# A two-layer hybrid decoder step: decode and projection buffers shared slot by slot, and other places in the order for steps of the mixers

## Chip, core and metric

The kernel runs on one core of a Trainium2 chip. The metric is the device time of one execution in microseconds (us). Engines: PE (TensorE, matmuls; PEld its weight loads), DVE (VectorE), ACT (ScalarE), POOL (GpSimd), SP (SyncE, which issues nearly all DMAs here; SPq is its queue).

## What is computed

One inference step of a two-layer trunk: 1024 prompt tokens and 8 sequences of 4 new tokens each. In each layer

```python
proj = x @ w_in                       # one input projection, 46 chunks of 128 columns here
# SSD (Mamba-2, 16 heads), MLA (latent attention, 8 heads, 8192 cached rows for each of the 8 sequences), GDN (gated DeltaNet, 4 heads)
mix = jnp.concatenate([y_ssd, y_mla, y_gdn], axis=-1)          # width 2048
x_new = layer_norm(DEEPNORM_ALPHA * x + mix @ w_out, ln_g, ln_b)
```

All of it is float32. The large products (input projection, q and kv of MLA, output projection) are three matmuls on a high and a low part of each operand: a `split` is a cast on ACT (high part) and a subtraction (low part) on DVE or POOL.

## The kernel before

Tokens are columns, in three blocks of 384, 384 and 288. Each layer has two phases.

**Phase 1** (`phase1`) interleaves three generators on PE: stream a (MLA norms, two GDN heads, one SSD group), stream b (layer norm of the input, two GDN heads, the sample's GDN, the other SSD group) and a filler (input projection, then `mla_q`, `mla_kv`, `absorb`). `merge` writes PE's order out by hand: a step that yields a number asks to be resumed that many us of the planner's PE clock (`self.clock`) later, a step that yields a set waits for those chunks, and the filler runs whenever no stream is due. The other engines' orders are made by a list scheduler (program order as priority, by its own estimates); `high_priority` moves what is traced inside it ahead. Queues of all engines are in order. PSUM banks in phase 1: `pj` 2 (filler), `a` 3, `b` 3.

Steps the change touches in phase 1: `rstd` (second half of a norm, two matmul groups with DVE and POOL L318 between), `gdn_block` (chains of small products whose results DVE takes from PSUM: L153, L829, L836), `ssd` (B and C products, copied out by ACT at L1024), `ssd_sample` (state update, first of eight after `stack`), `mla_q` (loads latents into `cq`; `product` writes bank `pj`; results go to DRAM as `qd`), and the end of the filler: `mla_prompt` loads queries for the attention, `absorb` loads `w_ukT` and four pieces of `qd` and makes the decode's queries, `mla_kv` makes keys and values.

**Phase 2** (`phase2`) first weaves the decode (32 units: gather 256 KB of rope rows and 2 MB of latents through POOL's queue, transpose them on DVE, scores `ps_dS`, softmax, `ps_dV`) with the prompt's attention (`mla_prompt`, banks `aS`, `aT`, `aO`); `weave_decode` fixes the orders of PE and DVE: every yield of the decode is a number of us for which attention steps run. `decode_end` joins the parts of the decode. Then the output projection `out_proj`: for each block of tokens 8 chunks of 48 matmuls, each chunk with two halves of weights `wo` (512 KB each, split), and 16 pieces `mix` (split) for the block; `ps_m` has 3 banks, `wo` 5 buffers of which a chunk uses 4. A `layer_norm` follows each block. The decode's buffers are one pool, the projection's another that takes the same memory after the first is closed. What attention is left after the decode is woven with the first block's projection (`weave`, 0.7 us of projection for 1 us of attention).

Of the kernel before, what the change touches and what calls it, by code (L numbers as in the profile page):

```python
# [33 lines left out]
SHARE2 = 0.7  # L34
# [93 lines left out]
class Builder:  # L128
# [177 lines left out]
    def rstd(self, T, tag, ss, n, mul, eps, soon=contextlib.nullcontext):  # L306
# [12 lines left out]
        yield 2.98  # L319
# [198 lines left out]
    def phase1(self, l):  # L518
# [3 lines left out]
        with self.pool(f"p1{l}") as p, self.psum_pool(f"p1ps{l}", pj=2, a=3, b=3):  # L522
# [32 lines left out]
            def fill():  # L555
# [27 lines left out]
            a = Stream([{0}], misc, self.gdn_head("a", 0), self.gdn_head("a", 2), self.mla_in("a"), self.ssd("a", 0))  # L583
# [116 lines left out]
    def gdn_block(self, r, L, T, Q, h, nb, x, S, ahead):  # L700
# [121 lines left out]
        for c, w in enumerate(ws):  # L822
# [6 lines left out]
            nc.vector.tensor_copy(out=vn, in_=p[:, :128])  # L829
# [5 lines left out]
            if S is None:  # L835
                nc.vector.tensor_copy(out=Sn, in_=p[:, :128])  # L836
            else:
                e = (16 + h) * 16 + cc + c
                self.stt(Sn, S, self.elast[:, e:e + 1], p[:, :128], ALU.mult, ALU.add)
# [5 lines left out]
        yield 5.2  # L845
# [160 lines left out]
    def ssd(self, r, g):  # L1006
# [9 lines left out]
        for t0 in (0, 4, 8):  # L1016
            p, p2 = self.psum(r), self.psum(r)
# [5 lines left out]
            if t0 < 8:  # L1023
                nc.scalar.copy(out=Bt[:, t0 * 128:t0 * 128 + 512], in_=p)  # L1024
                self.tt(nc.vector, CB[:, t0 * 128:t0 * 128 + 512].rearrange("p (c n) -> p c n", c=4), p2.rearrange("p (c n) -> p c n", c=4),
                        self.const[:, C_INC:C_INC + 128].unsqueeze(1).to_broadcast([128, 4, 128]))
            else:
                nc.scalar.copy(out=Bt[:32, 1024:1152], in_=p[:32, :128])
                self.tt(nc.vector, CB[:32, 1024:1056], p2[:32, :32], self.const[:32, C_INCS:C_INCS + 32])
# [107 lines left out]
    def ssd_sample(self, r, X, T, g, CT, Bt, CB, acc, big):  # L1137
# [55 lines left out]
        for b in range(8):  # L1193
            if b == 4:
                old((6, 7))
            yield 2.03
# [57 lines left out]
    def mla_q(self, cq, rot, ck, T):  # L1254
# [12 lines left out]

        def product(w, nb):
            n = BLOCKS[nb][1]
            ps = self.psum("pj")  # L1270
# [131 lines left out]
    def phase2(self):  # L1402
        l = self.l
        last = l == DEPTH - 1
        W, mla = self.regA[:, 0:4672], self.mla
        with self.psum_pool(f"p2ps{l}", aS=2, aT=2, aO=1):
            with self.pool(f"p2d{l}") as pd, self.psum_pool(f"p2dp{l}", dV=1) as ps:
                kts = self.hole.tile([128, 4224], F32, name="dec_k", tag="hole", bufs=1)

                V = {k: pd.tile([128, 4096], F32, name=f"dec_v{k}") for k in (2, 0, 1)}  # L1410
                self.RV = itertools.cycle([V[k] for k in range(3)])
                dec = self.decode(Ring(pd.tile([128, 8304], F32, name="dec")), kts, ps)
                self.weave_decode(dec, mla)
            with self.pool(f"p3{l}") as p3, self.psum_pool(f"p3ps{l}", m=3):

# [4 lines left out]
                ws = self.out_weights(itertools.cycle(rw), Ring(self.regA, 4672))  # L1420
                Rt = self.cso[:, 0:384]
                Ry = [p3.tile([128, 3072], F32, name="y"), W[:, 1536:4608]]
# [3 lines left out]
                self.pkv.close()  # L1426
                if not last:
                    self.take_x(l + 1)
                T = Ring(W, 0, 1536)
                Rx = Ring(self.tq(F32))  # L1430
                par = self.par[l]
                for nb in range(3):
                    if nb:
                        x2 = nb == 2 and not last
                        y = self.mix_load(Rx, Rm, None if x2 else Ry[nb % 2], None if x2 else Rt, nb)
                        out = self.out_proj(ws, nb, *y)
                    for _ in out:
                        pass
                    if last or nb < 2:
# [543 lines left out]
```

## Time and profile before

| | us |
|---|---|
| median of 3 runs | 3574.2 (3568.78 to 3581.75) |
| profiled execution, its time | 3572.76 |
| profiled execution, its span from first to last instruction | 3571.0 |
| PE busy | 3124.5 |
| mean granted PE clock | 0.939 of 2.4 GHz |
| layer 0: phase 1, decode, projection | 0 to 1060, 1060 to 1540, 1540 to 1800 |
| layer 1: phase 1, decode, projection | 1800 to 2816, 2816 to 3300, 3300 to 3555 |

A row of a timeline gives start, length, engine, line and operation as out<-in, with the number of merged instructions; a bracket gives the idle time before it and what ended that. A row of waits gives the engine and its line, what it waited for, us in total, times, and the longest.

### The profile page before, as it was taken

What the parts mean: (1) busy time and instruction counts of PE and PEld (TensorE: products, weight loads), DVE (VectorE), ACT (ScalarE), POOL (GpSimd) and SP (SyncE); (2) the same over time, 40 slices, a digit from 0 to 9 for tenths busy, and PEclk for the clock granted to TensorE, in tenths of its full rate; (3) what the DMA queues carried; (4) which work ended last, traced back from release to release, by engine and by line L of the source; (5) the groups of instructions that cost most, each with busy time, mean ns of one, the idle gap of its engine ahead of it and who ended that gap; (6) DMA issues with size and microseconds to landing.
All of it is one profiled execution on the core that took longest, in us unless ns stands there. A gap on an engine that the chain in (4) does not pass through costs nothing. (4 is left out here: it accounts for less than half of the span.)

```text
span 3571.0 us, 82553 instructions
## 1 busy us (share of the span) xinstructions
PE 3124.5 (87%) x33880; PEld 2666.9 (75%) x33880; DVE 2234.9 (63%) x4646; ACT 1337.2 (37%) x3099; POOL 1124.5 (31%) x1214
## 2 busy tenths in 40 slices
PE   6889999888778988979979999898987788889797
PEld 5888988888665655559878899887886566556697
DVE  7766365687545766745586653657865466666455
ACT  5433234333133344434434332343322343434344
POOL 4434344644421211101134444355453111211000
PEclk7999999999888999989989999999998799999898
DMA  3322324555776655444424232255567755553453
GB/s 137 123 90 88 106 67 161 168 169 177 249 251 201 207 178 191 171 154 157 151 83 126 83 94 90 68 171 184 173 214 254 230 191 190 183 196 128 161 180 127
DMA packets 317070, 564.70 MB, mean 158 GB/s; under 512 B 51772, under 2 KB 218748, under 8 KB 299668
## 3 DMA queue, kind: packets, MB, share of 16 engines
q1 hardware_dynamic: 293140, 408.42, 35.9%
q0 software_dynamic: 23552, 151.01, 12.0%
q8 instruction: 266, 4.36, 0.5%
q14 instruction: 112, 0.92, 0.1%
HBM read 429.00 MB, written 130.30 MB: 157 GB/s over the span
## 5 line engine op out<-in xcount | busy, mean ns | idle before, releaser
L180 PE MATMUL ps_pj<-xh,w_r 128*128 128x384 f32 (+1 forms) x4416 | 1212.7, 342 | 50.8 <-ACT p_cv L471 17.2
L180 PEld LDWEIGHTS ps_pj<-xh,w_r 128*128 128x128 f32 x4416 | 816.1, 196 | 71.0 <-ACT p_cv L471 19.1
L180 PE MATMUL ps_pj<-xl,w_r 128*128 128x384 f32 (+1 forms) x2208 | 733.9, 332 | 4.6 <-POOL xl L153 4.0
L180 PEld LDWEIGHTS ps_pj<-xl,w_r 128*128 128x128 f32 x2208 | 432.4, 196 | 13.5 <-POOL xl L153 11.1
L180 PE MATMUL ps_m<-mix,wo 128*128 128x384 f32 (+1 forms) x2304 | 395.4, 333 | 44.1 <-DVE wo L153 19.3
L180 PEld LDWEIGHTS ps_m<-mix,wo 128*128 128x128 f32 x2304 | 385.4, 196 | 50.8 <-DVE wo L153 22.4
L156 DVE SCALAR_TENSOR_TENSOR p_cv<-p_cv,c 128x384 f32<-128x384 f32 (+1 forms) x432 | 335.0, 779 | 71.9 <-ACT p_cv L159 65.9
L180 PE MATMUL ps_dS<-dec_k,c 32*32 32x256 f32 x8192 | 314.7, 385 | 31.5 <-issue 12.8
L153 POOL TENSOR_TENSOR w_r<-w_raw,w_r 128x1024 fp32r<-128x1024 f32 (+1 forms) x98 | 233.2, 2379 | 293.5 <-ACT w_r L165 251.3
L180 PEld LDWEIGHTS ps_dS<-dec_k,c 32*32 32x32 f32 x8192 | 190.1, 106 | 135.7 <-issue 85.0
L1667 DVE STREAM_TRANSPOSE dec_k<-dec_v 128x2048 f32<-128x2048 f32 x128 | 290.9, 2282 | 0.1
L1643 POOL DMA_INDIRECT dec<-cache_k_rope,c x64 | 60.9, 951 | 566.0 <-DVE dec L1736 516.9
L153 DVE TENSOR_TENSOR wo<-c,wo 128x1024 fp32r<-128x1024 f32 x96 | 119.0, 1243 | 128.2 <-PE ps_m L180 98.3
L159 ACT ACTIVATE p_cv<-p_cv 128x384 f32<-128x384 f32 x144 | 72.8, 505 | 314.8 <-DVE p_cv L156 313.8
L1470 ACT COPY c<-ps_aT 128x512 f32<-128x512 f32 (+3 forms) x192 | 89.9, 478 | 248.0 <-PE ps_aT L150 241.2
L165 ACT CAST wo<-c 128x1024 fp32r<-128x1024 f32 x96 | 100.4, 1050 | 218.3 <-DMA c<-w_out 174.9
L1643 POOL DMA_INDIRECT dec_v<-cache_kv_latent,c x128 | 120.8, 943 | 182.9 <-PE ps_dV L180 157.6
L180 PE MATMUL ps_b<-p_b 128*128 128x128 f32 (+7 forms) x1476 | 156.8, 284 | 21.1 <-ACT p_b L1024 8.4
L1513 DVE TENSOR_REDUCE c<-ps_aS 128x1 f32<-128x512 f32 (+3 forms) x192 | 105.4, 549 | 101.7 <-PE ps_aS L180 96.3
L159 ACT ACTIVATE c<-ps_aS,c 128x512 f32<-128x512 f32 (+3 forms) x192 | 110.6, 576 | 153.7 <-DVE c L1514 138.6
L318 POOL TENSOR_TENSOR c<-c,c 128x3 f32<-128x3 f32 (+2 forms) x22 | 17.1, 783 | 472.6 <-DVE c L317 472.6
L180 PEld LDWEIGHTS ps_b<-p_b 128*128 128x128 f32 (+5 forms) x1476 | 133.6, 161 | 37.7 <-ACT p_b L1024 9.9
(325 smaller groups left out, 5601.6 us busy)
## 6 DMA issues: line engine op xcount, KB each, us to landing
c<-w_out SPq DMA_DIRECT2D x96, 512.0 KB
w_raw<-w_in SPq DMA_DIRECT2D x92, 512.0 KB
pd<-p_cv SPq DMA_DIRECT2D x164, 192.0 KB
p_b<-pd SPq DMA_DIRECT2D x66, 256.0 KB
c<-pd SPq DMA_DIRECT2D x64, 256.0 KB
q<-rowd SPq DMA_DIRECT2D x48, 256.0 KB
p_b<-rowd SPq DMA_DIRECT2D x48, 256.0 KB
pd<-p_cv SPq DMA_DIRECT2D x82, 144.0 KB
```

The costliest lines, as they stand in the source:

```text
L153: eng.tensor_tensor(out=out, in0=a, in1=b, op=op)
L156: self.nc.vector.scalar_tensor_tensor(out=out, in0=a, scalar=s, in1=b, op0=op0, op1=op1)
L159: self.nc.scalar.activation(out=out, in_=in_, func=func, **kw)
L165: self.nc.scalar.copy(out=hi, in_=src)
L180: return self.nc.tensor.matmul(out, lhsT=lhsT, rhs=rhs, start=start, stop=stop)
L318: nc.gpsimd.tensor_tensor(out=r[:p, u], in0=r[:p, u], in1=self.mhalf[:p, 0:1].to_broadcast([p, u.stop - u.start]), op=ALU.pow)
L1470: nc.scalar.copy(out=t[:, :w], in_=p[:, :w])
L1513: nc.vector.reduce_max(out=m, in_=ps[:, :w], axis=AX.X)
L1643: nc.gpsimd.indirect_dma_start(out=out, out_offset=None, in_=src, in_offset=bass.IndirectOffsetOnAxis(ap=idx[:, c:c + 1], axis=0))
L1667: nc.vector.transpose(T[r].rearrange("p j s k -> p j (s k)"), V[:, :, r * 128:r * 128 + 128])
```

## The change

- `rstd`, the last step of `gdn_block`, the first state update of `ssd_sample` and the second and third group of `ssd` yield larger numbers, so their next PE instructions are put later in PE's order. DVE and ACT instructions of the GDN chains and of `ssd` get high priority.
- `mla_q` loads two blocks of latents before the rotation table; its products alternate between banks `pj` and `a`.
- `absorb` starts (and loads) before `mla_prompt`; the filler waits there until stream a has ended.
- In phase 2 one pool holds slots v0, v1, v2, d1, d2, d3. The projection's tiles take a slot each: `wo` takes v2, `mix` v0, v1 and d1, `y` takes d2. The first two halves of `w_out` are loaded (through `tok`) and split after unit 29, the first five `mix` after unit 30, eleven after the last; these splits subtract on POOL. The decode's first three loads come together, with no attention before the first unit.
- An attention step counts for at least 0.45 us in `weave_decode`. `decode_end` is woven with attention and the projection's first chunk. `ps_m` uses the banks of `dS` and `dV`, later of `aS` too. `wo` has 4 buffers in place of 5, its raw loads 3 in place of 2, its later splits high priority.

```diff
-        yield 2.98
+        yield 5.5
...
-            while due > 0 and next(second, self) is not self:
+            while due > 0:
+                if next(second, self):
+                    break
                 due, t = due - (self.clock - t), self.clock
...
-                    due -= self.clock - t
+                    due -= max(self.clock - t, 0.45)
...
+                yield {"a"}
+                absorb = self.absorb()
+                next(absorb)
                 self.mla = self.mla_prompt(self.tq(F32R), self.regA[:, 0:4672])
                 next(self.mla)
-                absorb = self.absorb()
-                next(absorb)
...
-            a = Stream([{0}], misc, self.gdn_head("a", 0), self.gdn_head("a", 2), self.mla_in("a"), self.ssd("a", 0))
+            def end():
+                self.done.add("a")
+                yield from ()
+            a = Stream([{0}], misc, self.gdn_head("a", 0), self.gdn_head("a", 2), self.mla_in("a"), self.ssd("a", 0), end())
...
-            self.tt(nc.vector, c3(Xc), c3(p), mk1(C_L1 + 32 * lv))
+            with self.tc.high_priority():
+                self.tt(nc.vector, c3(Xc), c3(p), mk1(C_L1 + 32 * lv))
...
-            self.tt(nc.vector, Tc, Tc, p, ALU.subtract)
-            nc.vector.transpose(Uc, Tc)
+            with self.tc.high_priority():
+                self.tt(nc.vector, Tc, Tc, p, ALU.subtract)
+                nc.vector.transpose(Uc, Tc)
...
-            nc.vector.tensor_copy(out=vn, in_=p[:, :128])
+            with self.tc.high_priority():
+                nc.vector.tensor_copy(out=vn, in_=p[:, :128])
...
+            with self.tc.high_priority():
+                if S is None:
+                    nc.vector.tensor_copy(out=Sn, in_=p[:, :128])
+                else:
+                    e = (16 + h) * 16 + cc + c
+                    self.stt(Sn, S, self.elast[:, e:e + 1], p[:, :128], ALU.mult, ALU.add)
...
-        yield 5.2
+        yield 7.5
...
         for t0 in (0, 4, 8):
+            if t0:
+                yield 2.5
             p, p2 = self.psum(r), self.psum(r)
...
+            with self.tc.high_priority():
+                if t0 < 8:
+                    nc.scalar.copy(out=Bt[:, t0 * 128:t0 * 128 + 512], in_=p)
+                    self.tt(nc.vector, CB[:, t0 * 128:t0 * 128 + 512].rearrange("p (c n) -> p c n", c=4), p2.rearrange("p (c n) -> p c n", c=4),
...
-            yield 2.03
+            yield 2.03 if b else 7.0
...
+        banks = itertools.cycle(("pj", "a"))
         def product(w, nb):
             n = BLOCKS[nb][1]
-            ps = self.psum("pj")
+            ps = self.psum(next(banks))
...
-        tables = {2: table(2, self.cst[:, 0:288], self.cst[:, 288:576]), 0: table(0, rot[:, 0:384], self.cso)}
+        tables = {2: table(2, self.cst[:, 0:288], self.cst[:, 288:576])}
         yield {"latents"}
-        for nb in (2, 0, 1):
-            latents(nb)
+        latents(2)
+        latents(0)
+        tables[0] = table(0, rot[:, 0:384], self.cso)
+        latents(1)
...
-        with self.psum_pool(f"p2ps{l}", aS=2, aT=2, aO=1):
-            with self.pool(f"p2d{l}") as pd, self.psum_pool(f"p2dp{l}", dV=1) as ps:
-                kts = self.hole.tile([128, 4224], F32, name="dec_k", tag="hole", bufs=1)
-                V = {k: pd.tile([128, 4096], F32, name=f"dec_v{k}") for k in (2, 0, 1)}
-                self.RV = itertools.cycle([V[k] for k in range(3)])
-                dec = self.decode(Ring(pd.tile([128, 8304], F32, name="dec")), kts, ps)
-                self.weave_decode(dec, mla)
-            with self.pool(f"p3{l}") as p3, self.psum_pool(f"p3ps{l}", m=3):
-                wo = lambda k: p3.tile([128, 1024], F32R, name=f"wo{k}")
-                rw = [wo(k) for k in range(4)]
-                Rm = itertools.cycle([p3.tile([128, 384], F32R, name=f"mix{k}") for k in range(32)])
-                rw.append(wo(4))
...
-                y = self.mix_load(None, Rm, Ry[0], Rt, 0)
-                out = self.out_proj(ws, 0, *y)
-                self.weave(mla, out, SHARE2)
...
+        with self.psum_pool(f"p2ps{l}", aS=2, aT=2, aO=1, dV=1) as ps, self.pool(f"p2d{l}") as pd:
+            kts = self.hole.tile([128, 4224], F32, name="dec_k", tag="hole", bufs=1)
+            place = lambda t, n, dt, name: pd.tile([128, n], dt, name=name, tag=t, bufs=1)
+            self.RV = itertools.cycle([lambda k=k: place(f"v{k}", 4096, F32, "dec_v") for k in range(3)])
+            d1, d2, d3 = (Ring(place(f"d{k}", n, F32, f"dec{k}")) for k, n in ((1, 4616), (2, 3072), (3, 608)))
+            d = {"T": [kts[:, r * 2048:r * 2048 + 2048].rearrange("p (j s k) -> p j s k", j=16, s=4) for r in range(2)],
+                 "gs": kts[:, 4096:4224], "ps": ps, "W": Ring(kts, 0, 4096)}
...
+            def projection():
+                rw = place("v2", 4096, F32R, "wo")
+                ws = self.out_weights(itertools.cycle([rw[:, k:k + 1024] for k in range(0, 4096, 1024)]), Ring(self.regA, 4672))
+                first = [next(ws), next(ws)]
+                yield
+                Rm, mix = [], [[], []]
+                for t, n, k0, k1 in (("v0", 4096, 0, 5), ("v1", 4096, 5, 10), ("d1", 4616, 10, 16)):
+                    m = place(t, n, F32R, "mix")
+                    Rm += [m[:, k * 384:k * 384 + 384] for k in range(2 * (k1 - k0))]
+                    self.mix_part(None, iter(Rm[2 * k0:]), 0, range(k0, k1), mix, nc.gpsimd)
+                    if t == "v0":
+                        yield
+                d.update(Rm=itertools.cycle(Rm), mix=mix, ws=itertools.chain(first, ws))
+            d["projection"] = projection()
+            self.weave_decode(itertools.chain(self.decode_setup(d1, d2, d3, d), self.decode_units(d)), mla)
+            next(d["projection"], None)
+            ws, Rm, y = d["ws"], d["Rm"], [d["mix"]]
+            two = lambda: ps.tile([128, 1024], F32, name="ps_m", tag="dS", bufs=1)
+            self.ms = itertools.cycle([two, lambda: self.psum("dV")])
+            def tail():
+                for _ in self.decode_end(d):
+                    for _ in itertools.islice(mla, 4):
+                        yield
+                Ry[0] = place("d2", 3072, F32, "y")
+                y.extend(self.mix_rest(Ry[0], Rt, 0))
+                yield from mla
+            out = self.out_proj(ws, 0, y)
+            self.weave(tail(), out, SHARE2)
+            self.pkv.close()
+            if not last:
+                self.take_x(l + 1)
+            T = Ring(W, 0, 1536)
+            Rx = Ring(self.tq(F32))
+            self.ms = itertools.cycle([two, lambda: self.psum("aS"), lambda: self.psum("dV"), lambda: self.psum("aS")])
+            par = self.par[l]
+            for nb in range(3):
+                if nb:
+                    x2 = nb == 2 and not last
+                    y = [self.mix_part(Rx, Rm, nb, range(16), [[], []], nc.vector)]
+                    y.extend(self.mix_rest(None if x2 else Ry[nb % 2], None if x2 else Rt, nb))
+                    out = self.out_proj(ws, nb, y)
+                for _ in out:
+                    pass
+                if last or nb < 2:
+                    finish(self.layer_norm("aT", T, y[1], nb, par[:, P_LNG:P_LNG + 8], par[:, P_LNB:P_LNB + 8], last,
+                                           self.total("aT", y[1], y[2]), Ry[nb % 2][:, :8 * BLOCKS[nb][1]]))
...
+    def decode_setup(self, D1, D2, D3, d):
...
-        vs, p5, O, m, al, sm, q4 = (D(n) for n in (256, 256, 2048, 32, 32, 32, 512))
+        (O, wv), (vs, p5, m, al, sm) = (D2(n) for n in (2048, 1024)), (D3(n) for n in (256, 256, 32, 32, 32))
         cks, krs, st = self.cso[:, 0:64], self.cso[:, 64:96], self.cso[:, 96:112]
-        d["load"], d["wv"] = self.decode_load(Ring(D(1536))), D(1024)
-        d["D"] = D.rest()
+        d["load"], d["wv"] = self.decode_load(Ring(D1(1536))), wv
+        q4 = D1(512)
+        d["D"] = D1.rest()
         d["ready"] = [d["load"](0, 0)]
-        yield 2.0
         self.dma(q4, self.qxd.rearrange("p r n -> p (r n)"))
         self.dma(cks.rearrange("p (r n) -> p r n", r=2), self.cks)
         self.dma(krs[0:32], self.krd[:, SEQ:NT])
         self.dma(d["gs"].rearrange("p (k n) -> p k n", k=4), self.gated[:, :, SEQ:NT])
         self.dma(d["wv"], self.i["w_uv"][l])
-        d["ready"] += [d["load"](0, 1)]
-        yield 2.0
-        d["ready"] += [d["load"](0, 2)]
+        d["ready"] += [d["load"](0, 1), d["load"](0, 2)]
+        yield 0.0
...
+            V, rr = next(RV)(), RR(512)
...
+            if k in (29, 30):
+                next(d["projection"])
...
-        W = Ring(d["D"].a, d["D"].base, d["D"].size)
+        W = d["W"]
...
+    def mix_part(self, Rs, Rm, nb, ks, mix, eng):
         c0, n, _ = BLOCKS[nb]
...
+        for k in ks:
             hi, lo = next(Rm)[:, :n], next(Rm)[:, :n]
             raw = Rs(384)[:, :n] if Rs else lo.bitcast(F32)
             self.dma(raw, self.mixd[:, k, c0:c0 + n])
             with self.tc.high_priority() if nb else contextlib.nullcontext():
-                self.split(None, raw, n, hi, lo, self.nc.vector)
+                self.split(None, raw, n, hi, lo, eng)
             mix[0].append(hi)
             mix[1].append(lo)
...
+        for k in range(48):
+            hi, lo = next(Rw), next(Rw)
+            raw = self.tok[:, :1024] if k < 2 or k % 3 == 0 else Rr(1024)
+            c, hf = k // 2 % 8, k % 2
+            self.dma(raw, self.i["w_out"][self.l, c, :, hf * 1024:hf * 1024 + 1024])
+            with self.tc.high_priority() if k > 1 else contextlib.nullcontext():
+                w = self.split(None, raw, None, hi, lo, self.nc.vector if k > 1 else self.nc.gpsimd)
+            yield w
...
+    def out_proj(self, ws, nb, parts):
         n = BLOCKS[nb][1]
+        mix = parts[0]
         for c in range(8):
             w = [next(ws), next(ws)]
-            ps = self.psum("m")
+            ps = next(self.ms)()
             for k in range(16):
                 hi, lo = w[k // 8]
                 s = slice((k % 8) * 128, (k % 8) * 128 + 128)
                 self.mm3(ps[:, :n], (hi[:, s], lo[:, s]), (mix[0][k], mix[1][k]), k == 0, k == 15)
                 yield
+            while len(parts) < 3:
+                yield True
+            y, total = parts[1:]
             self.stt(y[c], y[c], ALPHA, ps[:, :n], ALU.mult, ALU.add)
```

## Rows read from the trace of the kernel before

**Rows 1.** The page's first part: busy time and share of the span by engine.
```profile
PE 3124.5 (87%) x33880; PEld 2666.9 (75%) x33880; DVE 2234.9 (63%) x4646; ACT 1337.2 (37%) x3099; POOL 1124.5 (31%) x1214
```

**Rows 2.** Six stretches: length, busy PE, PEld, DVE, ACT, POOL (instructions), PEclk, DMA, GB/s.
```profile
1530.00:1640.00 110.00, 89.91 (x606) 75.77 (x591) 46.07 (x115) 37.99 (x64) 0.00 (x0) 0.88 0.47 162
3290.00:3400.00 110.00, 91.20 (x636) 76.58 (x621) 46.30 (x117) 38.40 (x64) 0.00 (x0) 0.89 0.44 152
1030.00:1110.00 80.00, 58.10 (x586) 42.72 (x587) 31.04 (x82) 27.49 (x81) 13.63 (x15) 0.77 0.69 211
2785.00:2870.00 85.00, 61.94 (x628) 45.64 (x626) 34.99 (x88) 28.98 (x85) 14.06 (x16) 0.74 0.69 208
940.00:1030.00 90.00, 70.35 (x409) 59.80 (x408) 52.58 (x107) 25.79 (x53) 33.27 (x38) 0.92 0.84 285
2695.00:2785.00 90.00, 69.16 (x385) 58.90 (x384) 50.06 (x103) 24.75 (x50) 29.63 (x35) 0.89 0.83 277
```

**Rows 3.** Waits of PE over the whole run: us in total, times, longest.
```profile
PE ps_m L180 <- DVE wo L153: 19.3, 10, 4.6
PE ps_pj L180 <- DMA cq<-cqd: 19.2, 4, 9.2
PE ps_a L180 <- ACT c L1024: 18.7, 2, 9.5
PE ps_a L180 <- DVE c L153: 18.4, 2, 9.5
PE ps_m L180 <- ACT mix L165: 17.9, 2, 9.9
...
PE ps_a L180 <- DVE p_sa L153: 15.3, 10, 5.3
...
PE ps_pj L180 <- DVE stage L153: 10.5, 7, 3.2
PE ps_b L180 <- DVE p_sb L153: 10.5, 12, 2.1
...
PE ps_a L180 <- DVE p_sa L829: 8.5, 6, 3.3
...
PE ps_b L180 <- ACT p_b L1024: 8.4, 2, 4.2
...
PE ps_a L150 <- DVE q L153: 7.0, 4, 3.3
...
PE ps_b L180 <- POOL p_b L318: 5.5, 4, 2.7
```

**Rows 4.** Timeline at the end of layer 0's decode: start, length, engine, line, operation, [idle before].
```profile
1556.15 9.32 PE L180 MATMUL ps_dV<-dec 128*32 128x256 f32 x32
...
1571.31 10.73 SPq L136 DMA_DIRECT2D mix<-mixd  x16
1578.12 8.33 ACT L165 CAST mix<-mix 128x384 fp32r<-128x384 f32 x16 [8.81 <-DMA mix<-mixd]
1578.66 8.38 DVE L153 TENSOR_TENSOR mix<-mix,mix 128x384 fp32r<-128x384 f32 x16 [7.29 <-ACT mix L165]
```

**Rows 5.** Timeline between phase 1 and decode, layer 0.
```profile
1025.06 8.34 SPq L136 DMA_DIRECT2D q<-qd  x14
...
1039.86 7.00 PE L180 MATMUL ps_a<-c 64*128 64x32 f32 x32 [8.93 <-DVE c L153]
...
1041.69 1.22 POOL L1643 DMA_INDIRECT dec_v<-cache_kv_latent,c  x1 [1.42 <-DMA c<-gated]
...
1060.89 0.95 POOL L1643 DMA_INDIRECT dec<-cache_k_rope,c  x1 [16.74 <-PE ps_aS L180]
```

**Rows 6.** Timeline of SP's queue where the MLA latents are loaded, layer 0.
```profile
966.90 0.51 SPq L136 DMA_DIRECT2D rot<-rotq  x1
967.47 4.70 SPq L136 DMA_DIRECT2D cq<-cqd  x6
```

**Rows 7.** One group by line: a 384-column subtraction on POOL, busy and mean ns.
```profile
L153 POOL TENSOR_TENSOR xl<-p_b,xh 128x384 fp32r<-128x384 f32 (+1 forms) x32 | 32.9, 1058 | 14.2 <-ACT xh L165 14.2
```

More of the change, by code (lines that the diff above doesn't have):

```diff
@@ L834, in gdn_block @@
             Sn = Q(128)
[L835 to L839, printed above, removed]
+            with self.tc.high_priority():
[4 more added lines that the diff above has]
+                    self.stt(Sn, S, self.elast[:, e:e + 1], p[:, :128], ALU.mult, ALU.add)
             S = Sn
@@ L1402, in phase2 @@
     def phase2(self):
-        l = self.l
+        nc, l = self.nc, self.l
         last = l == DEPTH - 1
         W, mla = self.regA[:, 0:4672], self.mla
-        with self.psum_pool(f"p2ps{l}", aS=2, aT=2, aO=1):
-            with self.pool(f"p2d{l}") as pd, self.psum_pool(f"p2dp{l}", dV=1) as ps:
-                kts = self.hole.tile([128, 4224], F32, name="dec_k", tag="hole", bufs=1)
-                V = {k: pd.tile([128, 4096], F32, name=f"dec_v{k}") for k in (2, 0, 1)}
-                self.RV = itertools.cycle([V[k] for k in range(3)])
-                dec = self.decode(Ring(pd.tile([128, 8304], F32, name="dec")), kts, ps)
-                self.weave_decode(dec, mla)
-            with self.pool(f"p3{l}") as p3, self.psum_pool(f"p3ps{l}", m=3):
-                wo = lambda k: p3.tile([128, 1024], F32R, name=f"wo{k}")
-                rw = [wo(k) for k in range(4)]
-                Rm = itertools.cycle([p3.tile([128, 384], F32R, name=f"mix{k}") for k in range(32)])
-                rw.append(wo(4))
-                ws = self.out_weights(itertools.cycle(rw), Ring(self.regA, 4672))
-                Rt = self.cso[:, 0:384]
-                Ry = [p3.tile([128, 3072], F32, name="y"), W[:, 1536:4608]]
-                y = self.mix_load(None, Rm, Ry[0], Rt, 0)
-                out = self.out_proj(ws, 0, *y)
-                self.weave(mla, out, SHARE2)
[L1426 to L1439, printed above, removed]
-                        finish(self.layer_norm("aT", T, y[1], nb, par[:, P_LNG:P_LNG + 8], par[:, P_LNB:P_LNB + 8], last,
-                                               self.total("aT", y[1], y[2]), Ry[nb % 2][:, :8 * BLOCKS[nb][1]]))
@@ L1577, in mla_prompt @@
         yield from pend
-    def decode(self, D, kts, ps):
-        d = {"T": [kts[:, r * 2048:r * 2048 + 2048].rearrange("p (j s k) -> p j s k", j=16, s=4) for r in range(2)],
-             "gs": kts[:, 4096:4224], "ps": ps}
-        yield from self.decode_setup(D, d)
-        yield from self.decode_units(d)
-        yield from self.decode_end(d)
-    def decode_setup(self, D, d):
+    def decode_setup(self, D1, D2, D3, d):
         nc, l = self.nc, self.l
-        vs, p5, O, m, al, sm, q4 = (D(n) for n in (256, 256, 2048, 32, 32, 32, 512))
+        (O, wv), (vs, p5, m, al, sm) = (D2(n) for n in (2048, 1024)), (D3(n) for n in (256, 256, 32, 32, 32))
         cks, krs, st = self.cso[:, 0:64], self.cso[:, 64:96], self.cso[:, 96:112]
-        d["load"], d["wv"] = self.decode_load(Ring(D(1536))), D(1024)
-        d["D"] = D.rest()
+        d["load"], d["wv"] = self.decode_load(Ring(D1(1536))), wv
+        q4 = D1(512)
+        d["D"] = D1.rest()
         d["ready"] = [d["load"](0, 0)]
-        yield 2.0
         self.dma(q4, self.qxd.rearrange("p r n -> p (r n)"))
@@ L1645, in load @@
         def load(b, u):
-            V, rr = next(RV), RR(512)
+            V, rr = next(RV)(), RR(512)
             for x in range(2):
@@ L1821, in decode_end @@
         self.dma(self.mixd[:, 8:12, SEQ:NT], y.rearrange("p (k n) -> p k n", k=4))
-    def mix_load(self, Rs, Rm, Ry, total, nb):
+    def mix_part(self, Rs, Rm, nb, ks, mix, eng):
         c0, n, _ = BLOCKS[nb]
-        mix = [[], []]
-        for k in range(16):
+        for k in ks:
             hi, lo = next(Rm)[:, :n], next(Rm)[:, :n]
@@ L1831, in mix_load, with mix_rest @@
             with self.tc.high_priority() if nb else contextlib.nullcontext():
-                self.split(None, raw, n, hi, lo, self.nc.vector)
+                self.split(None, raw, n, hi, lo, eng)
             mix[0].append(hi)
             mix[1].append(lo)
+        return mix
+    def mix_rest(self, Ry, total, nb):
+        c0, n, _ = BLOCKS[nb]
         if Ry is None:
@@ L1842, in mix_load @@
             y = [y[:, c] for c in range(8)]
-        return mix, y, total[:, :n]
+        return y, total[:, :n]
     def out_weights(self, Rw, Rr):
-        def load(c):
-            for hf in range(2):
-                raw = Rr(1024)
-                self.dma(raw, self.i["w_out"][self.l, c, :, hf * 1024:hf * 1024 + 1024])
-                yield self.split(None, raw, None, next(Rw), next(Rw), self.nc.vector)
-        for k in range(24):
-            yield from load(k % 8)
-    def out_proj(self, ws, nb, mix, y, total):
+        for k in range(48):
[7 more added lines that the diff above has]
+    def out_proj(self, ws, nb, parts):
         n = BLOCKS[nb][1]
+        mix = parts[0]
         for c in range(8):
             w = [next(ws), next(ws)]
-            ps = self.psum("m")
+            ps = next(self.ms)()
             for k in range(16):
```

12 lines of the change are left out of this document (5 added, 7 removed).

## Prediction

> **What bounds the kernel now.** I read the page first, then the run in equal stretches, then what PE waited for, then the timeline at each border of a stage. PE is busy 3124.5 us of 3571.0 [rows 1]; apart from its own weight loads no engine passes 63%. PE's order is written by hand in phase 1 and in the decode, so a wait at its head is lost unless a later one shrinks. 447 us of the span are PE's waits, and they gather at borders [rows 2]: at the end of the decode PE idles 110 - 89.9 = 20.1 us in layer 0 and 110 - 91.2 = 18.8 in layer 1; at its start 80 - 58.1 = 21.9 and 85 - 61.9 = 23.1; where the MLA queries are made 90 - 70.4 = 19.7 and 90 - 69.2 = 20.8. That is 124 us in 565 us. The same rows show a granted clock of 0.74 to 0.92, between the levels of 1.2 and 2.4 GHz: the busy part would have been shorter at the full clock by about busy times (1 - clock), 10.8 + 10.0 at the decode's end, 13.4 + 16.1 at its start, 5.6 + 7.6 at the queries. The reader should see in rows 3 that many of these waits have one cause and come twice, once for each layer: each is one place in an order.
>
> **The change, part by part.** Sums are for both layers, against the profiled execution of 3572.76 us (span 3571.0).
>
> *A, from decode to projection.* Before, the 16 `mix` loads (SP issues for 10.73 us) and their splits start only when the decode's pool is free, and PE waits for the first, 17.9 us in both layers [rows 3, 4]. After, two `wo` halves and five `mix` pieces are made during the last two units, and eleven follow while PE has attention, the 9.32 us of `decode_end` products [rows 4] and the five ready pieces. By the planner's clock the floor of 0.45 us and the 8 us that `decode_end` no longer claims leave about 26 us of attention per layer behind the decode, where before it ran out there. Moving the subtraction to POOL costs 1.06 us a piece [rows 7] for 8.38 / 16 = 0.52 on DVE [rows 4]: the eleven take 11 x 1.06 = 11.7 us, covered by those 26 us; without the cover, 11 x 0.54 = 6 us a layer. Bounds: nothing to all 38.9 us. I take 26, as `y` and the last pieces still come late. The clock gives back up to 20.8; I take 6.
>
> The Trainium skill (SBUF — State Buffer, Who interferes with whom) speaks against POOL here: a DVE instruction with two SBUF inputs and a GpSimd one that reads SBUF lock each other out for a whole instruction. By that rule the small DVE steps of `decode_end` could stand still for the 11.7 us of each layer, 23 us in all; attention on PE would hide it, and no row of this trace shows such a lock.
>
> *B, from phase 1 to decode.* SP issues 14 query loads for 8.34 us before what `absorb` needs, and PE waits 8.93 us for it [rows 5], 18.4 in both layers [rows 3]. After, `absorb` is asked for first; most of that goes. The first gather of rope rows waited 16.74 us for the last matmul with the kv weights [rows 5], whose memory it took; in slot d1 it does not. The first unit no longer stands behind 4 us of planned attention. Against that, stream b's last steps come later and the first gather, issued at 1041.69 when b's memory came free [rows 5], with them: three norms and a state update, 3 x 2.52 + 4.97 = 12.5 us by the planner. Bounds: from a loss of 25 us (12.5 each) to a gain of all 45.0. I take 16 and 8 of the clock's 29.5. The wait for stream a costs nothing: its memory's last reader in layer 0 lies well ahead of `absorb`, and if it did not, the price is that distance.
>
> *C, queries of MLA.* The rotation table stands in SP's queue just ahead of the six latent loads [rows 6], and its place is memory of the last projection block. Loading two blocks first can start them while that block still runs: up to the 19.2 us of waits for `cq` [rows 3]. Two more banks remove up to the 10.5 us of waits for `stage` [rows 3]. The DMA engines are 0.84 busy there [rows 2], so I take 16 of 40.5 us; bounds 0 and 40.5.
>
> *D, the rest of phase 1.* ACT's copy at L1024 stands behind activations that wait for DVE, and PE waits 18.7 + 8.4 = 27.1 us [rows 3]. High priority and 2.5 us between the groups: 20, bounds 0 and 27. The first state update of the sample waits for `stack`, longest 5.3 in the row of 15.3 [rows 3]; 7 of two such. Norms and GDN's last step: 7.0 + 5.5 [rows 3], I take 6. GDN's chains: 8.5 + 10.5 [rows 3]; high priority for them delays conv steps on the same DVE, so -10 to 19, and I take 5. In all 38.
>
> *E, the projection's weights.* PE waits 19.3 us for `wo` [rows 3]. Three raw buffers and priority help, four `wo` buffers in place of five hurt: a half can be split only after its last reader. That is a cast and a subtraction in the time of 24 matmuls. Bounds -10 and 19; I take 4.
>
> Added instructions: none of weight; DMAs, splits and matmuls are the same in number.
>
> **The sum.** 32 + 24 + 16 + 38 + 4 = 114. In a fixed order a wait that is removed lets PE reach the next unready operand sooner. I let a quarter come back so, 28. 3572.8 - 86 = 3486.8; the median of the runs shown is 1.4 above the profiled execution, so 3488.
>
> **Rivals.**
>
> *Transfers bind the end of phase 1.* For it: DMA 0.83 to 0.84 and 277 to 285 GB/s there [rows 2]; the loads cannot come sooner if the engines are full. B and C give nothing, D half: 32 + 19 + 4 = 55, less a quarter, 41: 3533. Chance 0.24.
>
> *The early splits come no earlier.* The change to the decode's end does nothing, if the list scheduler places loads and splits of `mix` and `wo` behind the decode anyway or `decode_end` still holds DVE: A falls out. 82 - 20 = 62: 3512. For it: the 16 pieces are bound by one queue before [rows 4]; against it: the slots free one after another. Chance 0.13.
>
> *The clock comes back whole.* The rows with idle gaps are those with low clock [rows 2]; if the gaps close and the clock holds at its upper level in A and B, 50.3 come back in place of 14: 3452. Chance 0.12. The Trainium skill (TensorE: Matmul & The Clock Gate, What's actually happening) says the clock follows how busy PE has been, which agrees with these rows.
>
> *Slower: the streams set the end of phase 1.* Every later place lengthens a stream. For b that is, by the planner, 4 x 2.3 for GDN, 5 for the products of `ssd`, 12.5 at its end, and 2.52 for each norm of the input (three in layer 0, one in layer 1): 34 and 29 us. If the filler runs out first, PE idles for it; B, C and D are lost, A and E give 36 x 3/4 = 27: 3572.8 - 27 + 63 + 1.4 = 3610. It decides where more than 1060.9 - 1041.7 = 19 us of it arrive at the end, the distance between the gather that needed b's memory and the one that needed the filler's last matmul [rows 5]. Against it: SSD pairs wait for their chunks anyway, which absorbs what was added before them. Chance 0.09.
>
> *The forecast:* 0.39, its own range 3465 to 3515. The other 0.03 goes to gains and losses that cancel.
>
> **Range and chances.** From 3440 to 3558: below lies a bit of the clock's case with C whole, above the slower one and part of the first rival. About 0.3% (11 us) is what a measurement of this kernel can tell from no change. Faster: 0.39 + 0.12 + 0.13 + 0.24 less a few hundredths of the rivals that end near the old time, 0.86; same 0.05; slower 0.09.
>
> **What would show it.** A: after the last `ps_dV` of a layer's decode, `ps_m` begins within some 5 us, mixed with attention, and the wait of `ps_m` for `mix` is under 5 us a layer. B: PE's wait for `absorb` is under 3 us, and the first `ps_dS` follows the last kv matmul within 5 us. C: `cq` loads are issued ahead of `rot`, while the last block's projection still runs. D: PE's waits on L1024 are gone. E: waits for `wo` no longer than before. It is wrong if PE idles longer just before the first `ps_dS`, if phase 1 ends later than 1060 and 1016 us after its start, or if the decode's units, with less attention between them, keep their length, so that the attention moved behind them is added and not moved.

## Result and profile after

The changed kernel takes 3527.5 us (median of 4 runs, 3523.1 to 3532.9), the kernel before in the same series 3571.5 (3563.2 to 3581.8): a ratio of 0.988, 95% interval 0.985 to 0.991. The forecast was 3488 with a range of 3440 to 3558. The sign was right, and the gain is 44 us where 86 were expected. The profiled execution has a span of 3523.2 us, mean granted clock 0.949 (before 0.939).

The page's first part, as in [rows 1]:
```profile
PE 3110.6 (88%) x33880; PEld 2635.1 (75%) x33880; DVE 2215.6 (63%) x4610; ACT 1325.8 (38%) x3099; POOL 1166.3 (33%) x1250
```
The stretches of [rows 2], moved to where the same work stands now (decode's end and decode's start, layer 0 and layer 1 of each), under a row for the first 1000 us:
```profile
0.00:1000.00 1000.00, 877.75 (x7582) 812.78 (x7582) 642.19 (x1313) 359.91 (x857) 453.90 (x490) 0.95 0.44 140
1520.00:1630.00 110.00, 105.44 (x765) 84.60 (x744) 50.03 (x153) 56.63 (x117) 15.55 (x16) 0.97 0.48 152
3251.00:3361.00 110.00, 105.94 (x748) 85.31 (x733) 52.34 (x154) 57.32 (x118) 15.47 (x16) 0.97 0.44 140
1030.00:1110.00 80.00, 52.37 (x631) 36.87 (x634) 30.69 (x69) 14.57 (x44) 19.64 (x29) 0.77 0.70 237
2760.00:2845.00 85.00, 57.34 (x729) 39.81 (x729) 31.14 (x69) 14.85 (x45) 19.52 (x29) 0.78 0.71 243
```
The same row for the first 1000 us before:
```profile
0.00:1000.00 1000.00, 875.48 (x7563) 807.66 (x7563) 648.97 (x1326) 359.60 (x851) 459.35 (x503) 0.94 0.44 142
```
At the decode's end PE now idles 4.6 and 4.1 us, where [rows 2] had 20.1 and 18.8. At its start it idles 27.6 and 27.7, more than the 21.9 and 23.1 of before. At the queries (920 to 1010 and 2650 to 2740 now) PE is busy 70.76 and 69.84 of 90 us, so it idles 19.2 and 20.2, after 19.7 and 20.8. In the first 1000 us PE idles 122.3 us, after 124.5 before: what was removed there came back as other waits.

Waits of PE over the whole run, to be held against [rows 3]:
```profile
PE ps_dS L180 <- issue: 38.0, 7, 18.4
...
PE ps_pj L180 <- DMA cq<-cqd: 18.7, 4, 9.1
...
PE ps_b L180 <- ACT p_b L1040: 4.0, 4, 1.5
...
PE ps_m L180 <- DVE y L156: 1.3, 2, 0.6
```
`ps_m` waits for neither `mix` nor `wo` (17.9 and 19.3 before). The 27.1 us on L1024 (now L1040) are 4.0. The wait for `cq` is untouched. New at the top is `ps_dS`: two of its seven waits, of about 18 us each, stand ahead of the first one of a layer. The view puts them to no instruction; the timeline shows what they are.

Timeline of layer 0 around the start of the decode, the place of [rows 5]:
```profile
1054.46 1.55 PE L180 MATMUL ps_a<-w_r,ck 128*128 128x512 f32 x6
...
1061.32 1.79 DVE L156 SCALAR_TENSOR_TENSOR p_b<-p_b,c,ps_b 128x288 f32<-128x288 f32 x4 [4.57 <-DMA p_b<-yd]
1061.87 1.79 SPq L136 DMA_DIRECT2D mixd<-p_b  x4
...
1066.25 1.22 POOL L1680 DMA_INDIRECT dec_v<-cache_kv_latent,c  x1 [8.18 <-issue]
...
1069.02 0.95 POOL L1680 DMA_INDIRECT dec<-cache_k_rope,c  x1 [0.30 <-issue]
...
1075.77 0.71 DVE L1759 STREAM_TRANSPOSE dec<-dec 128x512 f32<-128x512 f32 x1 [12.65 <-DMA dec<-cache_k_rope,c]
...
1076.58 1.10 PE L180 MATMUL ps_dS<-dec,c 32*32 32x256 f32 x16 [17.93 <-issue]
```
The last kv matmul ended at 1056. Stream b's last result is stored only at 1061.87, the first gather follows at 1066.25 (1041.69 in [rows 5]), and PE idles until the gathered rows are transposed. The view puts the idle time before the gather of layer 0 to no instruction. In the view of the tile `dec_v` over the whole run, the same idle time before the gather of layer 1 has the store by name:
```profile
  DMA mixd<-p_b: 8.2, 1
```
The rope gather follows the first one by 2.8 us; before, it was 19.2 us behind.

Each layer in three parts, read from the starts and ends in the timelines: phase 1 up to the first `ps_dS`, decode up to the end of the last `ps_dS`, projection up to the last matmul with `wo`. Layer 0 / layer 1, in us; "gather" is the first gather, counted from the start of the layer. The last column is the ratio of the timed runs to the kernel before on the same chip.

| kernel | gather | phase 1 | decode | projection | ratio |
|---|---|---|---|---|---|
| before | 1041.7 / 997.6 | 1075.2 / 1031.5 | 455.8 / 459.9 | 269.2 / 258.8 | 1 |
| after | 1066.2 / 1023.1 | 1076.6 / 1033.9 | 444.3 / 444.3 | 252.2 / 251.4 | 0.988 |
| e5 (after, again) | 1067.3 / 1026.0 | 1077.8 / 1036.4 | 445.2 / 444.3 | 252.2 / 246.8 | 0.9885 |
| e6 | 1067.0 / 1021.3 | 1078.8 / 1033.2 | 446.4 / 446.8 | 252.2 / 250.0 | 0.9872 |
| e7 | 1048.8 / 1004.2 | 1061.6 / 1016.2 | 447.8 / 446.3 | 249.2 / 247.1 | 0.9753 |
| e8 | 1064.0 / 1023.1 | 1074.7 / 1033.6 | 446.8 / 448.4 | 251.8 / 250.0 | 0.9879 |
| e1 | 1046.2 / 991.6 | 1064.8 / 1010.0 | 408.5 / 407.4 | 251.2 / 251.0 | 0.9763 |
| e2 | 1067.4 / 1020.3 | 1079.7 / 1033.0 | 429.0 / 429.0 | 265.4 / 257.9 | 1.0054 |
| e4 | 1068.2 / 1016.7 | 1095.5 / 1044.8 | 410.8 / 410.3 | 247.6 / 239.2 | 0.9902 |
| e9 (e3, again) | 1044.2 / 992.5 | 1057.5 / 1006.8 | 410.4 / 405.4 | 251.6 / 246.8 | 0.9736 |
| e10 | 1043.0 / 993.0 | 1057.2 / 1005.9 | 422.6 / 424.1 | 230.3 / 228.3 | 0.9691 |
| e11 | 1074.3 / 1029.9 | 1084.5 / 1041.9 | 407.0 / 409.3 | 251.8 / 250.6 | 0.9895 |
| e12 | 1041.0 / 997.7 | 1059.6 / 1016.3 | 408.0 / 408.3 | 251.9 / 249.8 | 0.9747 |

From before to after: phase 1 +1.4 + 2.4, decode -11.5 - 15.6, projection -17.0 - 7.4, in all -47.7 of the spans' -47.8. All of the gain lies behind the first `ps_dS`.

The chips differ: before takes 3572 to 3579 us where before, after and e5 to e8 were run, and 3504 and 3499 us where e1 to e4 and e9 to e12 were. On the latter the decode is some 27 to 41 us shorter in each layer with the same phase 2 (last section). So ratios are compared, and small differences only between kernels that ran on one chip: e1 to e4, e5 to e8, e9 to e12.

### The profile page after: what moved, and what is told of

It is laid out like the page before. It is cut to its first block, busy times and chain, and to the rows that moved or that the text cites. A ratio compares the mean times of both kernels' runs of the same rounds, so it can differ in the third digit from the quotient of the medians.

```text
span 3523.2 us, 82464 instructions
## 1 busy us (share of the span) xinstructions
PE 3110.6 (88%) x33880; PEld 2635.1 (75%) x33880; DVE 2215.6 (63%) x4610; ACT 1325.8 (38%) x3099; POOL 1166.3 (33%) x1250
## 5 line engine op out<-in xcount | busy, mean ns | idle before, releaser
L156 DVE SCALAR_TENSOR_TENSOR p_cv<-p_cv,c 128x384 f32<-128x384 f32 (+1 forms) x432 | 342.9, 797 | 89.8 <-ACT p_cv L159 83.2
L180 PE MATMUL ps_dS<-dec_k,c 32*32 32x256 f32 x8192 | 330.3, 385 | 24.6 <-DVE dec_k L1704 7.9
L180 PEld LDWEIGHTS ps_dS<-dec_k,c 32*32 32x32 f32 x8192 | 182.7, 106 | 152.9 <-issue 101.9
L180 PE MATMUL ps_b<-p_b 128*128 128x128 f32 (+7 forms) x1476 | 163.2, 289 | 39.8 <-DVE p_b L153 17.9
L180 PE MATMUL ps_aS<-mix,wo 128*128 128x384 f32 (+1 forms) x960 | 157.4, 321 | 0.0
L180 PEld LDWEIGHTS ps_aS<-mix,wo 128*128 128x128 f32 x960 | 152.3, 188 | 1.2
L1717 DVE TENSOR_REDUCE dec<-ps_dS 128x1 f32<-128x512 f32 x64 | 44.3, 692 | 169.5 <-PE ps_dS L180 169.5
```

Source lines behind the costliest of these rows:

```text
L156: self.nc.vector.scalar_tensor_tensor(out=out, in0=a, scalar=s, in1=b, op0=op0, op1=op1)
L180: return self.nc.tensor.matmul(out, lhsT=lhsT, rhs=rhs, start=start, stop=stop)
L1717: nc.vector.tensor_reduce(out=al, in_=s3, axis=AX.XY, op=ALU.max)
```

## Experiments

**e1, phase 1 as before, phase 2 as changed** (every phase 1 hunk of the diff undone).

> Phase 1 as before, phase 2 as changed. Theory (the whole gain is at the border from decode to projection, and the edits of phase 1 give nothing net because stream b's later end delays the first gathers): 3505 to 3527 us, no slower than the whole change; the first gather of latents is back near 1042 us and PE's idle time just before the first ps_dS is under 10 us in each layer. Rival (the edits of phase 1 carry about half of the gain of 44 us, and the border to the projection the other half): about 3548 us.

Measured: 3418.9 against 3504.2 us, ratio 0.9763 [0.9735, 0.9792] (95% interval, here and below). Phase 2 alone gives more than the whole change gave in either series. The rival is out. The idle time before the first `ps_dS` is gone: PE goes from the last kv matmul straight to it. The first `ps_dS` comes 10.4 and 21.5 us earlier than in the kernel before, whose trace is from another chip.

**e2, phase 1 as changed, phase 2 as before.**

> Phase 1 as changed, phase 2 as before. Theory: 3561 to 3582 us, no difference from before that can be measured; PE waits about 20 us or more before the first ps_dS. Rival (the edits of phase 1 carry half of the gain): about 3549 us.

Measured: 3521.9 against 3504.2 us, 1.0054 [1.0034, 1.0074]. The phase 1 edits by themselves cost 18 us. The theory that they are neutral was too mild, and that they carry half of the gain is out. PE waits only 2.3 and 3.2 us just before the first `ps_dS`, not the 20 expected: phase 2 as before plans attention there.

**e3, the four later places undone, the rest kept.**

```diff
-        yield 5.5
+        yield 2.98
-        yield 7.5
+        yield 5.2
-            if t0:
-                yield 2.5
-            yield 2.03 if b else 7.0
+            yield 2.03
```

> The whole change, but the four later places (the last step of rstd, the last step of a GDN block, the groups of ssd, the first state update of ssd_sample) are as before; priorities, banks, the order of the latents and of absorb stay. Theory: stream b ends about 25 us earlier, the first gather with it, and PE's 18 us before the first ps_dS shrink to under 8; some waits that the later places removed come back (stack, norms): 3500 to 3518 us. Rival (the later places save more in waits than they cost at the end): 3535 us or more.

Measured: 3406.5 us, 0.9717 [0.9689, 0.9745], against e1 0.9763 on the same chip: without the later places the rest of the phase 1 edits (priorities, banks, latents, absorb) saves 12 us (no run of e3 is as slow as any of e1). The first gather is at 1045.8, and the 18 us of idle time are gone. Priority alone does not remove the waits on L1024 (here L1038), which are 18.7 and 8.4 in [rows 3]:
```profile
PE ps_a L180 <- ACT c L1038: 18.4, 2, 9.2
```

**e4, attention for 8 us ahead of the first unit.**

```diff
-        yield 0.0
+        yield 8.0
```

> The whole change, but with attention for 8 us planned ahead of the decode's first unit. Theory (PE has nothing to do there but to wait for the first gathers): PE's wait before the first ps_dS falls from 18 to about 8 us in each layer and the same attention is missing behind the decode: 3507 to 3515 us. Rival (the decode's chain of units sets its length, and the attention behind it was already cover for the projection's first loads; or the first attention steps are not ready either): 3522 to 3535 us.

Measured: 3469.8 us, 0.9902 [0.9878, 0.9927]. The whole change itself was not run on this chip, so there is no base for what the 8 us are worth; the trace speaks against the theory. The first attention steps run, but a later one waits 12 us for query loads that SP issues only at 1069.95 us, behind the first gather (1068.19), and the first `ps_dS` now comes 27.3 us behind that gather, not 10.3. Waits over the whole run:
```profile
PE ps_aS L180 <- DMA q<-qd: 28.8, 4, 11.9
```

**e5, the whole change again, as the base of e6 to e8.**

> The whole change once more, beside the next three on one chip, since the chip of the first four runs was faster for the kernel before. If the chip is again the faster one, the score matmuls of the decode (ps_dS from dec_k) are busy about 250 us and not 330, and theory (most of what the four later places cost is PE's idle time before the first ps_dS, 18 us in each layer) says a ratio of 0.981 to 0.984; rival (the whole change keeps its ratio of the first chip): 0.987 to 0.989.

Measured: 3533.3 against 3578.7 us, 0.9885 [0.9851, 0.9919], as in the first series. It ran on a slower chip, with long score matmuls, so what the whole change gives on the faster one was not measured.

**e6, rstd and the first state update back; e7, GDN's last step and the groups of ssd back** (halves of e3's diff).

> The whole change, but the last step of rstd and the first state update of ssd_sample are back in their old places; GDN's last step and the groups of ssd stay late. Theory (it is the end of stream b that delays the gathers): nearly all that putting back four places gave, a ratio about 0.010 below that of the whole change. Rival (the middle of the streams counts as much, since every later step moves the end by its full amount): half of it, about 0.005 below.

> The whole change, but GDN's last step and the groups of ssd are back in their old places; rstd and ssd_sample stay late. Theory: within 0.003 of the whole change, since ssd pairs wait for their chunks, which absorbs what is added before them. Rival (every later step moves the end by its full amount): about 0.005 below.

Measured: e6 0.9872 [0.9840, 0.9904], no difference from e5; e7 0.9753 [0.9721, 0.9785], 45 us faster than e5. It is the other way round than theory had it: with the middle late, the places at the end of stream b cost nothing that can be measured, and those in its middle cost nearly all. The table shows it in the first gather: 1067.0 in e6, as in e5, and 1048.8 in e7. The end places are not free for that: in e7, where they alone are late, PE still idles 13.4 and 12.6 us before the first `ps_dS`, and in e3 and e9, on other chips, not at all. What they cost there was not measured on one chip.

**e8, the first `wo` and `mix` splits after the last unit in the program.**

```diff
-            if k in (29, 30):
-                next(d["projection"])
...
-            next(d["projection"], None)
+            for _ in d["projection"]:
+                pass
```

> The whole change, but the first halves of w_out and the first mix pieces are loaded and split after the last unit of the decode, not after units 29 and 30. Theory (the early splits are what closes the gap behind the decode): PE waits for mix or wo again, some 10 to 20 us in each layer, a ratio 0.006 to 0.011 above that of the whole change. Rival (the attention moved behind the decode is cover enough by itself): within 0.002 of the whole change.

Measured: 3531.8 us, 0.9879 [0.9846, 0.9911]: no difference from e5. But the edit moved nothing. It changes where the splits stand in the program, and the orders of SP, ACT and POOL are made by the list scheduler. Loads of `w_out` and `mix` and splits of `mix` around the last `ps_dS` of layer 0 (its end: 1520.90 in after, 1521.46 in e8), in after:
```profile
1503.43 7.73 SPq L136 DMA_DIRECT2D c<-w_out  x2
1516.92 2.98 SPq L136 DMA_DIRECT2D mix<-mixd  x5
1520.19 3.04 POOL L153 TENSOR_TENSOR mix<-mix 128x384 fp32r<-128x384 f32 x3 [9.38 <-ACT mix L165]
```
and in e8:
```profile
1505.26 7.53 SPq L136 DMA_DIRECT2D c<-w_out  x2
1517.47 2.91 SPq L136 DMA_DIRECT2D mix<-mixd  x5
1521.16 3.88 POOL L153 TENSOR_TENSOR mix<-mix 128x384 fp32r<-128x384 f32 x4 [8.73 <-ACT mix L165]
```
The splits are as early in e8 as in after, so neither the theory nor the rival was tested.

**e9, e3 again, as the base of e10 to e12.**

> The whole change with all four later places as before, once more, as the base of the next three. With the score matmuls stretched as in the first profiles: the middle places were worth 0.0132 and the end places 0.0013, so a ratio of 0.973 to 0.976; with the short score matmuls of the first four runs, 0.970 to 0.973.

Measured: 3407.3 against 3498.8 us, 0.9736 [0.9712, 0.9761], on another of the faster chips.

**e10, e9 without the floor of 0.45 us.**

```diff
-                    due -= max(self.clock - t, 0.45)
+                    due -= self.clock - t
```

> As the base, but an attention step counts in the weave with the decode for what it takes, without the floor of 0.45 us. Theory (the attention moved behind the decode is the cover that closes the gap there, since the early splits were worth nothing): the decode is some 13 to 20 us longer in each layer and PE waits again behind it, a ratio 0.005 to 0.011 above the base. Rival (an attention step costs the same wherever it stands): within 0.002 of the base.

Measured: 3391.1 us, 0.9691 [0.9666, 0.9717]; its runs (3389.3 to 3399.7) lie below all of e9's (3400.6 to 3412.7). The theory falls with its sign. The decode is 12.2 and 18.7 us longer, the projection 21.3 and 18.5 shorter, and no matmul of the projection waits for `mix` or `wo` behind the decode. The floor costs some 16 us. e10 is the fastest version found, ahead of before and, by ratio, of the whole change.

**e11, e9 with GDN's last step late again.**

```diff
-        yield 5.2
+        yield 7.5
```

> As the base, but with the last step of a GDN block late again (7.5 in place of 5.2). Theory (six blocks of stream b, 2.3 us each, and the stream never catches up): stream b's end and the first gather come 12 to 19 us later, PE idles before the first ps_dS, a ratio 0.007 to 0.011 above the base. Rival (SSD pairs wait for their chunks anyway and absorb it, as the prediction had it): within 0.002 of the base.

Measured: 3464.7 us, 0.9895 [0.9871, 0.9919]: 57 us slower than e9 from one number. SP's queue shows stream b's stores; the fourth of GDN, the first of ssd and the last, in e9:
```profile
605.25 0.39 SPq L136 DMA_DIRECT2D mixd<-p_b  x1
...
760.23 0.32 SPq L136 DMA_DIRECT2D yd<-p_b  x1
...
1038.78 2.99 SPq L136 DMA_DIRECT2D mixd<-p_b  x4
```
and in e11:
```profile
628.32 0.41 SPq L136 DMA_DIRECT2D mixd<-p_b  x1
...
783.84 0.32 SPq L136 DMA_DIRECT2D yd<-p_b  x1
...
1068.31 1.87 SPq L136 DMA_DIRECT2D mixd<-p_b  x4
```
They are 23, 24 and 30 us later. What GDN lost is never caught up: the first gather, 1044.2 in e9, stands at 1074.3, and PE, which in e9 does not wait there, idles 18.9 us before the first `ps_dS`.

**e12, e9 with the old order of `mla_prompt` and `absorb`, and no wait for stream a.**

> As the base, but mla_prompt is started ahead of absorb as before, and the filler does not wait for stream a. Theory (absorb's wait of 5 us in each layer becomes 9 to 10 again and everything behind it moves by as much): a ratio 0.002 to 0.004 above the base. Rival (the loads of the attention's queries, now later, cost as much at the start of the decode): within 0.001 of the base, or below it.

Measured: 3412.8 us, 0.9747 [0.9723, 0.9771]; the intervals of e9 and e12 overlap. By the medians the old order costs 5.5 us, in theory's direction, but their runs overlap too, so this cannot be told from nothing. The absorb wait is 15.1 us against 10.1.

## Why the forecast was half right

**A, decode to projection: right, and more than forecast; which part of the change does it is not shown.** Idle time fell by 15.5 + 14.7 = 30.2 us (forecast 26). Busy times (1 - clock), as the prediction worked it, fell from 20.8 to 6.3, so 14.5 for the clock (forecast 6). `ps_m` begins 11 us after the last `ps_dS`, woven with attention. The prediction rested it on early splits, covered by attention that the floor moves behind the decode. The cover was not needed: e10 takes the floor away and gains. The early splits are there in every run with the new phase 2, e8 included: in layer 0 the first `mix` load starts 4.0 us before the last `ps_dS` ends, where before it started 40.3 us behind it. That is what the prediction said, and its rival that they come no earlier is out. But no run has the new phase 2 without them, so their part, that of the slots that come free one by one and that of `decode_end` woven in were not told apart.

**E, `wo`: under-sized.** The 19.3 us went whole; forecast 4. Which of the edits to `wo` did it was not tried.

**B, phase 1 to decode: the mechanism right, its price on the other side wrong.** From the first gather to the first `ps_dS` it was 33.5 and 33.9 us, now 10.3 and 10.8. Not all of that is slot d1 and the first unit's new place: in e2, without them, it is 12.3 and 12.7, since the late gather comes after the last kv matmul. What phase 2 gives here by itself e1 shows: the first `ps_dS` comes 10.4 and 21.5 us earlier. In the whole change this went to nothing, as the first gather came 24.6 and 25.5 us later; the filler's last kv matmul did not (1056.0, before 1060.6). PE's idle time just before the first `ps_dS`, a sign of being wrong by the prediction, rose from 1.2 us to 17.9 and 18.4, and the wait for `absorb`, to fall under 3 us, is 5.1 after 8.9. The prediction took it that the gathers hang on stream b's end; before, [rows 5] names another load (`c<-gated`), after, layer 1's gather names b's store. It charged them with b's last 12.5 us alone and let the rest be absorbed: "SSD pairs wait for their chunks anyway, which absorbs what was added before them". That step failed. e11 shows that nothing is absorbed, e6 and e7 that the middle counts for nearly all. The size was off as well: 4 x 2.3 = 9.2 us by the planner were 23 in e11 by the fourth store. PE's waits for GDN's states (`p_sb`) rise from 9.2 to 21.7 us between e9 and e11, a part of that; why later places make these chains wait longer stays open. The slower rival named this mechanism, at a chance of 0.09; it acts, and what phase 2 gives outweighs it: e7, with the middle places alone put back, takes 3488.4 us against 3578.7 on its chip, a gain of the size of the forecast.

**C: wrong.** The loads of `cq` do stand ahead of `rot` in SP's queue, but still behind the last projection block, whose matmuls end at about 943 and whose store is the first row here, and PE waits 18.7 us for them (19.2 before):
```profile
945.43 0.60 SPq L136 DMA_DIRECT2D gated<-p_cv  x1
946.43 2.60 SPq L136 DMA_DIRECT2D cq<-cqd  x4
949.13 1.00 SPq L136 DMA_DIRECT2D rot<-rotq  x1
950.17 1.78 SPq L136 DMA_DIRECT2D cq<-cqd  x2
```
They could not start while that block still ran, as the prediction had it; `rot`'s place was not what held them. Only the waits for `stage` fell, from 10.5 to 3.4 + 2.4, and not by the two more banks alone: e9, which has them too, waits 12.4.

**D: most waits right, the sum wrong.** The waits on L1024 fell from 27.1 to 4.0 in the whole change; e3 says by the later places and not by priority. Those for `stack` and GDN's chains fell as well, that of the norms (L318) did not: 5.5 before, 6.9 after. Yet PE idles as long in the first 1000 us as before (122.3, 124.5; 119.5 in e9). The quarter that was to come back was nearly the whole for these edits.

**A term that was missing.** The scores `ps_dS` from `dec_k` are busy 330.3 us after and 314.7 before, with the same instructions: 15.6 us that the decode's gain lacks. It fits that from e2 to e11, on faster chips, where these scores take as long (253.8 and 252.9), the decode falls by 22.0 and 19.7 us and not by 11.5 and 15.6. In sum B, C and D were to bring 78, less a quarter, and brought -3.8 with what remains of phase 1; A and E were to bring 36, less a quarter, and decode and projection brought 51.5. That the total fell inside the range is partly luck: a large miss on one side and a gain above the forecast on the other.

**The other rivals.** The time lies nearest to the rival of the transfers (3533), but e1 and e9 show that the first `ps_dS` can come sooner with the same transfers; for C alone it stays open, with the DMA engines 0.89 and 0.87 busy at the queries. The clock did not come back whole: busy times (1 - clock) at the decode's start fell from 29.5 to 24.7, so A and B got 19.3 of 50.3 back, where 14 were taken.

## What to carry to other kernels

In an order written by hand, a step that is put later can be paid in full at the end of its stream, unless the trace shows a wait further on that has slack: one number in the middle of a stream cost 57 us. Whether a removed wait was worth something is read from the idle time of the whole stage, not from its own row. A chain that frees memory for the next stage's first transfers is on the critical path, even where PE's own wait names nothing. Where a scheduler makes an engine's order, moving a line of the program need not move the work (e8): read from the trace that an experiment did what it was made for.

## What was not expected of the hardware

The same score matmuls are slower on some chips. The group of `ps_dS` by line (busy, mean ns), before, after and then e9:
```profile
L180 PE MATMUL ps_dS<-dec_k,c 32*32 32x256 f32 x8192 | 314.7, 385 | 31.5 <-issue 12.8 <-DVE dec_k L1667 10.6
```
```profile
L180 PE MATMUL ps_dS<-dec_k,c 32*32 32x256 f32 x8192 | 330.3, 385 | 24.6 <-DVE dec_k L1704 7.9 <-issue 1.7
```
```profile
L180 PE MATMUL ps_dS<-dec_k,c 32*32 32x256 f32 x8192 | 251.3, 380 | 26.9 <-DVE dec_k L1702 26.4 <-issue 0.5
```
One matmul takes as long, but they follow each other more slowly. In one unit of after, the first 64 take 3.69 us and the other 64 take 1.96; in the last unit of a layer, behind the last gather, all 128 take 3.66:
```profile
1254.38 3.69 PE L180 MATMUL ps_dS<-dec_k,c 32*32 32x256 f32 x64
...
1258.72 1.96 PE L180 MATMUL ps_dS<-dec_k,c 32*32 32x256 f32 x64
...
1517.25 3.66 PE L180 MATMUL ps_dS<-dec_k,c 32*32 32x256 f32 x128
```
In after the first 64 take 2.8 to 3.7 us in every unit but the last two of each layer, where they take 1.93, as nearly all do in e9. What holds them up is not shown; that only units with gathers still coming are slow points to the gathers.

The prediction found no row for a lock between DVE and POOL. After has one, while POOL subtracts the eleven `mix` pieces; POOL's row first, then DVE's:
```profile
1537.93 10.67 POOL L153 TENSOR_TENSOR mix<-mix 128x384 fp32r<-128x384 f32 x11 [10.96 <-ACT mix L165]
```
```profile
1528.19 0.16 DVE L153 TENSOR_TENSOR c<-c 128x2 f32<-128x2 f32 x1
...
1539.98 1.94 DVE L153 TENSOR_TENSOR c<-c 128x2 f32<-128x2 f32 x2 [1.02 <-ACT c L159]
1541.96 0.16 DVE L1570 RECIPROCAL c<-c 128x1 f32<-128x1 f32 x1
1542.15 0.74 DVE L1571 TENSOR_SCALAR c<-c 128x2 f32<-128x2 f32 x1
```
A TENSOR_TENSOR of this size takes 0.16 us alone and about 0.97 each here, as long as one of POOL's subtractions (10.67 / 11); the reciprocal with one input is not held up. For the TENSOR_TENSOR this agrees with the Trainium skill (SBUF — State Buffer, Who interferes with whom): two SBUF inputs on DVE and a GpSimd instruction that reads SBUF exclude each other for a whole instruction. The TENSOR_SCALAR in the last row takes 0.74 us, where the same one takes 0.21 at 1529.09, without POOL beside it. The three slow ones together cost some 2 us here, behind 7.5 us of `ps_dV` matmuls, and not the 11.7 us a layer that the prediction worked out from the rule.
